# A hybrid decoder trunk: pools re-laid so that matmul blocks begin on 2 KB boundaries in SBUF

## The chip, the cores and the metric

The kernel runs on one core of a Trainium2 chip. The metric is the device time of one execution in microseconds; the median of three runs stands for the kernel. One further execution was recorded by the hardware profiler, and its rows are the ones quoted here. The engines are PE (matrix products), DVE (vector), ACT (scalar), POOL (GpSimd) and SP, which here issues the DMAs.

## The reference

Two layers of a decoder trunk on x of 512 tokens by 1024 features, float32. Each layer normalises x, projects it once into everything that three token mixers need, runs the mixers, merges them through gates, projects the merged rows and adds them to x.

```python
h = rms_norm(x, pre_norm)
z_a, xbc, dt, u, z_b, q_lat, kv_lat, k_rope, z_c, gates = split_columns(h @ w_in)
a = ssd_branch(z_a, xbc, dt, ...) @ w_a        # causal conv, chunked state space scan, gate, norm
b = s5_branch(u, z_b, ...) @ w_b               # complex diagonal scan, gelu, GLU, gate
c = mla_branch(q_lat, kv_lat, k_rope, z_c) @ w_c   # causal attention, 16 heads
merged = sum(sigmoid(gate_i) * branch_i)
x = x + rms_norm(merged @ w_o, post_norm)
```

The SSD branch also uses the small tables `conv_w`, `conv_b`, `d_ssd` and `ssd_norm`, the GLU uses `b_glu`, the latents use `q_norm` and `kv_norm`.

## The kernel before

**Tiling.** Tokens lie along the free axis (512 of them, one PSUM bank), features on the 128 partitions. A float32 product is made of three: each operand is split into a high part `h` (rounded by ACT) and a low part `l` (the rest, by DVE or POOL), and PE forms high x high, high x low and low x high. `dense` does that for a bank: over the 128-row blocks of its input it issues L109 (`wh`, high part) and L110 (`wh`, low part) in turn, then L112 (`wl`, high part). With eight blocks a bank is 24 matmuls of 512 columns. The moving operand is the input block, 512 columns of 4 bytes, so 2 KB per partition: `hh`/`hl` for the normalised x, `ah`/`al` for the activations that the branches leave, `cqh`/`cql` for the MLA latents. The stationary operand is a block of 128 columns of `wh` or `wl`, 512 bytes. `mm3` (L54 to L56) issues the three products for one block; in the output projection it is the weights `woh`/`wol` that move and `ah`/`al` that are stationary. `weight` streams one 128 x 1024 block of weights into `wf`, ACT makes `wh` from it (L59) and DVE (L71) or POOL (L74) makes `wl`; each has two buffers.

**Stages.** In each layer: the norm, the first two tiles of the projection and the MLA branch with the preparation of the S5 matrices as filler work (to about 390 us in layer 0, 1390 in layer 1); the merges of `w_c` beside the S5 scan on DVE (to about 500); the SSD branch (to about 697); eight S5 blocks, each with a tile of the `w_a` merge, and the GLU (to about 885); the `w_b` merges with the loads of the output weights (to about 960); the output projection (to about 1010, and the end).

**What sets the order.** A scheduler orders the instructions of each engine by a simulation of its own, and waits are added to that order; each engine then runs its row in order. SP's DMA queue is such a row as well: a load that waits holds those behind it. Tiles come from pools, and a pool's place in SBUF follows from the pools opened before it. The pools of a stage (`mla`, `act`, `mg`, `dt`, `ssd`, `s5`, `wo`, `scan`) open and close and take over each other's space; a tile waits for the instructions that use the tiles whose addresses it takes over. A tile with a tag in a pool that stays open waits for the readers of the buffer's last holder alone.

**The names that the change touches.** `sm` is the pool of small tiles and stays open for both layers. `qn` and `kvn` are the norms' gains of the latents, `mx` and `nm` the row maxima of the attention; they are in the stage pool `mla`. `cw`, `cb`, `dsk`, `sn` (SSD) are in `mg`, loaded at L703 to L710, and `cw` and `cb` are halved by DVE. `bglu` (L940 to L942) is in `s5` and halved as well. `s5_block.load` (L892) brings a block's inputs `u` and its states `sdr` into a staging tile `uf` or `sf` of the pool `s5`, one buffer each. `tmp` is a pool tag with seven buffers of 128 x 512, used by all stages.

**Where blocks begin.** The addresses of the program before, in bytes past a 2 KB boundary, are: `wf`, `wh`, `wl`, `hh`, `hl` and the tiles of `kp`, `tp` 768; `act` (`ah`, `al`), `mg` and `mla` 640, with the latents' `cqh` and `cql` at 704; `dt` and `s5` 1024; `ssd` 384; `wo` 2016.

Of the kernel before, what the change touches and what calls it, by code (L numbers as in the profile page):

```python
# [9 lines left out]
F32 = mybir.dt.float32  # L10
# [7 lines left out]
L = 2  # L18
# [5 lines left out]
# first tile of each part of the input projection, in the host's order  # L24
ZA, XBC, UB, ZB, CQ, CKV, ZC, GT = 0, 8, 24, 32, 40, 44, 46, 54
SCALE = 96.0 ** -0.5
MAGIC = 12582912.0
SWAP16 = [(i + 16) % 32 for i in range(32)]
# [6 lines left out]
class Trunk:  # L35
    def __init__(self, ctx, tc, a, out, tap=None):
# [3 lines left out]
        self.const = pool("const")  # L40
        self.wp = pool("wp", 2)
# [3 lines left out]
        self.sm = pool("sm")  # L45
# [39 lines left out]
    def weight(self, src, n, pool=None):  # L85
        """hi and lo parts of a block of n columns per partition, streamed from DRAM"""
# [14 lines left out]
    def dense(self, src, rhs, m=P, n=None, main=True):  # L101
        """[m, T] bank of src^T rhs; rhs: (hi, lo) per 128 rows"""
# [12 lines left out]
    def proj2(self, l, tiles):  # L115
        """two tiles of the projection, first for the first half of the tokens"""
# [57 lines left out]
    def sincos_small(self, ang, n):  # L174
# [21 lines left out]
        # sin = 2 s c, cos = 1 - 2 s^2  # L196
# [8 lines left out]
    def rsqrt_mean(self, ss, n, scale, eps=EPS):  # L205
        """(scale * ss + eps) ** -0.5 on n columns"""
        v = self.sm.tile([P, n], F32, name="rs_v", tag=f"rsv{n}")
        r = self.sm.tile([P, n], F32, name="rs_r", tag=f"rsr{n}")
        self.ts(v, ss, scale, eps, ALU.mult, ALU.add)
        self.gt(r, v, self.mhalf[:, :n], ALU.pow)  # L210
        return r

    def rsqrt_rows(self, sq, scale):
        """sq [128, T]: sums over partitions -> (scale * sum + eps) ** -0.5 along T, on every partition"""
# [13 lines left out]
    def s5_prep(self, l, pp):  # L228
# [27 lines left out]
        # f = (abar - 1) / lambda  # L256
# [18 lines left out]
        # coefficients of the scan over blocks: groups 0..31 on the lower half, 32..63 on the upper  # L275
# [25 lines left out]
        def block(b):  # L301
            """inputs in blocks of 8 steps: (step, channel of the group) on partitions; what depends on B and C alone"""
# [49 lines left out]
        def back(b, s, uf, bb, v1, w1):  # L352
# [19 lines left out]
            if s % 2:  # L372
# [3 lines left out]
                # kernel of the steps within a block  # L376
# [32 lines left out]
    def norm_in(self, tt, xt, G):  # L409
        """RMS norm of a tile of tokens (two halves of its features), transposed and split into self.hh, self.hl"""  # L410
# [15 lines left out]
    def silu2(self, l, tile_, keep=True):  # L426
        """2 silu of a tile of the projection"""
# [24 lines left out]
    def merge(self, l, i, w, acts, m, rrow=None):  # L452
        """merged += 2 sigmoid(gate_i) * (w^T acts) (* rrow along T), a tile of it; its gates run ahead"""
# [15 lines left out]
    def mla(self, l, fill):  # L469
        nc, tc, a = self.nc, self.tc, self.a  # L470
        with tc.tile_pool(name=f"mla{l}", bufs=1, reuse_waits="tile") as mp:
            qn, kvn = mp.tile([P, 4], F32, name="qn"), mp.tile([P, 2], F32, name="kvn")
# [118 lines left out]
    def attend_qk(self, mp, q, k, h):  # L591
        """rows of exp(q k^T * SCALE - max), causal; their sums in self.rs"""
        nc = self.nc
        mx, nm = (mp.tile([P, 4], F32, name=x, tag=x, bufs=2) for x in ("mx", "nm"))
# [17 lines left out]
    def attend_v(self, mp, scs, v):  # L612
        """probabilities times v, transposed, as the sum of two parts of [64, T]"""
        nc = self.nc
        # key block kb holds queries kb * 128 ...
# [25 lines left out]
    def ssd_dt(self, l, sp):  # L641
        """dt, its cumulative decays and what depends on tokens and heads alone"""
        nc, a, sm = self.nc, self.a, self.sm
        raw = sp.tile([P, 512], F32, name="dtraw")
        self.act_(raw[32:48], self.krdt[32:48])
# [35 lines left out]
        cs2 = sp.tile([64, 512], F32R, name="cs2")  # L681
# [16 lines left out]
    def ssd(self, l):  # L698
        nc, tc, a = self.nc, self.tc, self.a
        with tc.tile_pool(name=f"ssd{l}", bufs=1, reuse_waits="tile") as sp:  # L700
            dt, cs, cs2, dte, dec = self.dts
            cw, cb = self.mgp.tile([P, 16, 4], F32, name="cw"), self.mgp.tile([P, 16], F32, name="cb")
# [4 lines left out]
            dsk, sn = self.mgp.tile([P, 8], F32, name="dsk"), self.mgp.tile([P, 8], F32, name="sn")  # L707
# [5 lines left out]
            def conv(t):  # L713
                """silu of the causal convolution of a tile of channels"""
# [499 lines left out]
```

## Time and profile before

| | us |
|---|---|
| runs | 2005.52, 2007.95, 2009.80 |
| median | 2007.95 |
| span of the profiled execution | 2005.7 |
| PE busy in it | 1890.3 |
| DVE busy in it | 1451.9 |
| ACT busy in it | 942.0 |
| POOL busy in it | 649.9 |

The span is the time from the first to the last instruction of the one profiled execution; the times of the runs also hold what lies around it. Matmuls are pipelined, so a matmul's duration in the timeline (0.39 us for 512 columns) is longer than the distance to the next one's start; what a stream of matmuls costs is read from the distance of the starts.

### The profile page before, as it was taken

What the parts mean: (1) busy time and instruction counts of PE and PEld (TensorE: products, weight loads), DVE (VectorE), ACT (ScalarE), POOL (GpSimd) and SP (SyncE); (2) the same over time, 40 slices, a digit from 0 to 9 for tenths busy, and PEclk for the clock granted to TensorE, in tenths of its full rate; (3) what the DMA queues carried; (4) which work ended last, traced back from release to release, by engine and by line L of the source; (5) the groups of instructions that cost most, each with busy time, mean ns of one, the idle gap of its engine ahead of it and who ended that gap; (6) DMA issues with size and microseconds to landing.
All of it is one profiled execution on the core that took longest, in us unless ns stands there. A gap on an engine that the chain in (4) does not pass through costs nothing.

```text
span 2005.7 us, 27806 instructions
## 1 busy us (share of the span) xinstructions
PE 1890.3 (94%) x9688; PEld 1524.2 (76%) x9688; DVE 1451.9 (72%) x2845; ACT 942.0 (47%) x1743; POOL 649.9 (32%) x743
## 2 busy tenths in 40 slices
PE   7897999899999989999997999998999999999998
PEld 6685777687877868887875777776878887788786
DVE  7866667699999857744478666677999996776433
ACT  4364566522555445533333655564235563554331
POOL 1855466301333201201118556662013331012010
PEclk9898999899999999999998999998999999999999
DMA  5232234232321266344232333342332224662531
GB/s 166 88 115 83 91 118 128 83 108 74 127 74 64 75 184 181 93 152 157 88 91 83 108 104 111 91 139 82 96 123 77 74 74 111 181 171 84 168 126 42
DMA packets 132605, 219.96 MB, mean 110 GB/s; under 512 B 36208, under 2 KB 75760, under 8 KB 131952
## 3 DMA queue, kind: packets, MB, share of 16 engines
q1 hardware_dynamic: 132464, 218.19, 35.4%
q8 instruction: 76, 1.25, 0.3%
q14 instruction: 65, 0.53, 0.1%
HBM read 182.08 MB, written 31.33 MB: 106 GB/s over the span
## 4 chain that ended last, share of the span: by engine, by line
PE 59%; DVE 25%; DMA 7%; POOL 3%; ACT 3%; issue 2%; SPq 1%; DVEq 0%; POOLq 0%; ACTq 0%
PE mm L109 14%; PE mm L110 13%; PE mm L112 13%; DVE wl L71 4%; DVE keep L62 3%; PE mm L54 2%; PE mm L55 2%; PE mm L56 2%; DMA wf<-in_w_in 2%; DVE ms L882 2%; DVE sc_t L879 2%; PE pk L378 2%; DVE ms L881 1%; PE aux L55 1%; PE aux L54 1%
## 5 line engine op out<-in xcount | busy, mean ns | idle before, releaser
L109 PE MATMUL mm<-hh,wh 128*128 128x512 f32 (+1 forms) x1232 | 501.2, 407 | 16.4 <-DVE ql L71 8.8
L110 PE MATMUL mm<-hl,wh 128*128 128x512 f32 (+1 forms) x1232 | 493.6, 401 | 0.0
L59 ACT ACTIVATE wh<-wf 128x1024 fp32r<-128x1024 f32 (+1 forms) x294 | 291.2, 994 | 423.7 <-PE mm L110 240.8
L71 DVE TENSOR_TENSOR wl<-wf,wh 128x1024 fp32r<-128x1024 f32 (+1 forms) x243 | 297.5, 1229 | 183.8 <-ACT wh L59 149.6
L112 PE MATMUL mm<-hh,wl 128*128 128x512 f32 (+1 forms) x1232 | 315.1, 393 | 2.4 <-DVE wl L71 2.4
L109 PEld LDWEIGHTS mm<-hh,wh 128*128 128x128 f32 (+1 forms) x1232 | 237.2, 193 | 78.6 <-ACT wh L59 10.0
L110 PEld LDWEIGHTS mm<-hl,wh 128*128 128x128 f32 (+1 forms) x1232 | 236.8, 192 | 50.2 <-issue 1.9
L112 PEld LDWEIGHTS mm<-hh,wl 128*128 128x128 f32 (+1 forms) x1232 | 227.5, 187 | 52.0 <-DVE wl L71 3.2
L74 POOL TENSOR_TENSOR mg<-mg,tmp 128x512 f32<-128x512 f32 x32 | 77.7, 2429 | 464.4 <-DVE tmp L71 242.7
L74 POOL TENSOR_TENSOR wl<-wf,wh 128x1024 fp32r<-128x1024 f32 (+1 forms) x51 | 109.5, 2147 | 292.2 <-PE mm L112 186.7
L109 PE MATMUL mm<-ah,wh 128*128 128x512 f32 x512 | 204.1, 401 | 0.1
L110 PE MATMUL mm<-al,wh 128*128 128x512 f32 x512 | 201.2, 394 | 0.0
L112 PE MATMUL mm<-ah,wl 128*128 128x512 f32 x512 | 130.8, 396 | 0.0
L109 PEld LDWEIGHTS mm<-ah,wh 128*128 128x128 f32 x512 | 96.2, 188 | 25.5 <-issue 1.8
L110 PEld LDWEIGHTS mm<-al,wh 128*128 128x128 f32 x512 | 96.2, 188 | 22.1 <-issue 0.5
L112 PEld LDWEIGHTS mm<-ah,wl 128*128 128x128 f32 x512 | 95.7, 188 | 22.6
L602 DVE CUSTOM_DVE_ANT_0 sc<-aux,cmask 128x128 f32<-128x128 f32 (+3 forms) x128 | 60.3, 486 | 50.8 <-PE aux L56 49.1
L59 ACT ACTIVATE sc<-sc,nm 128x128 f32<-128x128 f32 (+3 forms) x128 | 70.3, 553 | 30.3 <-DVE nm L66 30.2
L74 POOL TENSOR_TENSOR pv<-pq,ar 128x288 f32<-128x288 f32 x64 | 56.4, 903 | 85.3 <-PE pk L378 68.3
L71 DVE TENSOR_TENSOR pl<-aux,ph 128x512 fp32r<-128x512 f32 (+1 forms) x96 | 54.8, 594 | 26.2 <-ACT ph L59 25.7
L59 ACT ACTIVATE tmp<-mm 128x512 f32<-128x512 f32 x76 | 44.9, 594 | 60.6 <-PE mm L56 34.1
L62 DVE SCALAR_TENSOR_TENSOR keep<-mm,cw,keep 128x511 f32<-128x511 f32 (+2 forms) x96 | 71.1, 741 | 2.1 <-ACT keep L59 1.5
(344 smaller groups left out, 4079.9 us busy)
## 6 DMA issues: line engine op xcount, KB each, us to landing
wf<-in_w_in SPq DMA_DIRECT2D x156, 512.0 KB
odr<-pv SPq DMA_DIRECT2D x64, 128.0 KB
wf<-in_w_c SPq DMA_DIRECT2D x16, 512.0 KB
wf<-in_w_a SPq DMA_DIRECT2D x16, 512.0 KB
wf<-kpad SPq DMA_DIRECT2D x128, 64.0 KB
wf<-odr SPq DMA_DIRECT2D x16, 512.0 KB
wf<-in_w_glu SPq DMA_DIRECT2D x16, 512.0 KB
wf<-in_w_b SPq DMA_DIRECT2D x16, 512.0 KB
```

Source lines behind the costliest of these rows:

```text
L54: mm(out, ah, bh, start=start, stop=False)
L55: mm(out, ah, bl, start=False, stop=False)
L56: mm(out, al, bh, start=False, stop=stop)
L59: self.nc.scalar.activation(out, in_, func, **kw)
L62: self.nc.vector.scalar_tensor_tensor(out, in0, s, in1, op0, op1)
L71: self.nc.vector.tensor_tensor(out, a, b, op)
L74: self.nc.gpsimd.tensor_tensor(out, a, b, op)
L109: mm(ps[:m], wh[:, o(i)], bh, start=i == 0, stop=False)
L110: mm(ps[:m], wh[:, o(i)], bl, start=False, stop=False)
L112: mm(ps[:m], wl[:, o(i)], bh, start=False, stop=i == k - 1)
L378: nc.tensor.matmul(pk.rearrange("p g k -> p (g k)"), bbp[b % 2][:, q:q + 4].rearrange("p g h -> p (g h)"), v1[:, :, 0:8].rearrange("p g k ...
L602: nc.vector.tensor_tensor_reduce(out=sc, in0=ps[:, :n], in1=self.cmask[:, 512 - n:512], op0=ALU.add, op1=ALU.max, scale=1.0, scalar=-3.0e3 ...
```

## The change

The pool `sm` opens ahead of the large pools. A helper `align` takes a pad tile of a given number of float32 columns from a pool and clears one column of it; it is called in `sm` (200 columns), in the pool `dt` (160) and in `wo` (504). The small tiles `qn`, `kvn`, `mx`, `nm`, `cw`, `cb`, `dsk`, `sn` and `bglu` move from their stage pools into `sm`, each with a tag of its own, so layer 1 uses the same buffer as layer 0. The staging tile of `s5_block.load` becomes a `tmp`. `cs2` is taken from its pool earlier. Comments are dropped, which moves the line numbers.

```diff
         self.const = pool("const")
+        self.sm = pool("sm")
+        self.align(self.sm, PAD_LOW)
         self.wp = pool("wp", 2)
         self.hp = pool("hp")
         self.kp = pool("kp", 8)
         self.tp = pool("tp", 7)
-        self.sm = pool("sm")
...
+    def align(self, pool, n):
+        t = pool.tile([P, n], F32, name="pad", tag="pad")
+        self.nc.vector.memset(t[:, 0:1], 0.0)
...
-            qn, kvn = mp.tile([P, 4], F32, name="qn"), mp.tile([P, 2], F32, name="kvn")
+            qn, kvn = self.sm.tile([P, 4], F32, name="qn", tag="qn"), self.sm.tile([P, 2], F32, name="kvn", tag="kvn")
...
-        mx, nm = (mp.tile([P, 4], F32, name=x, tag=x, bufs=2) for x in ("mx", "nm"))
+        mx, nm = (self.sm.tile([P, 4], F32, name=x, tag=x, bufs=2) for x in ("mx", "nm"))
...
         raw = sp.tile([P, 512], F32, name="dtraw")
+        cs2 = sp.tile([64, 512], F32R, name="cs2")
+        self.align(sp, PAD_DT)
...
-            cw, cb = self.mgp.tile([P, 16, 4], F32, name="cw"), self.mgp.tile([P, 16], F32, name="cb")
+            cw, cb = self.sm.tile([P, 16, 4], F32, name="cw", tag="cw"), self.sm.tile([P, 16], F32, name="cb", tag="cb")
...
-            dsk, sn = self.mgp.tile([P, 8], F32, name="dsk"), self.mgp.tile([P, 8], F32, name="sn")
+            dsk, sn = self.sm.tile([P, 8], F32, name="dsk", tag="dsk"), self.sm.tile([P, 8], F32, name="sn", tag="sn")
...
-            f = sp.tile([P, 8, 64], F32, name=nm + "f", tag=nm + "f")
+            f = self.tmp().rearrange("p (g c) -> p g c", g=8)
...
-        bg = sp.tile([P, 8], F32, name="bglu")
+        bg = self.sm.tile([P, 8], F32, name="bglu", tag="bglu")
...
                 if m < 6:
                     w_out(wp, m)
+            self.align(wp, PAD_TOP)
```

By the addresses of the changed program, `wp`, `hp`, `kp`, `tp`, `act`, `mla`, `mg`, `dt`, `ssd`, `s5` and `wo` all begin at 0 past a 2 KB boundary, and so do their blocks of 2 KB. The pools of the S5 preparation and the scan stay where they were.

The scheduler makes new rows of this. At the start of the program DVE's row was, from the product `pq` of the first S5 tables on (`e_...` is an exponential on small tiles, `hl` the low part of the normalised x):

```order
L66 TENSOR_SCALAR pq_810<-bc_803,sgn 128x128
L66 TENSOR_SCALAR e_nf<-e_t 128x64
L62 SCALAR_TENSOR_TENSOR e_r<-e_nf,e_zc 128x64
L66 TENSOR_SCALAR e_t<-e_nf 128x64
L62 SCALAR_TENSOR_TENSOR e_r<-e_nf,e_r 128x64
L66 TENSOR_SCALAR e_t<-e_t 128x64
L66 TENSOR_SCALAR e_p<-e_r 128x64
L62 SCALAR_TENSOR_TENSOR e_p<-e_p,e_r 128x64 x5
L71 TENSOR_TENSOR hl<-aux,hh 128x4x128
```

and what stands behind `pq` is now:

```order
L75 TENSOR_SCALAR cw<-cw 128x64
L75 TENSOR_SCALAR cb<-cb 128x16
L75 TENSOR_SCALAR e_nf<-e_t 128x64
L71 SCALAR_TENSOR_TENSOR e_r<-e_nf,e_zc 128x64
L75 TENSOR_SCALAR e_t<-e_nf 128x64
L71 SCALAR_TENSOR_TENSOR e_r<-e_nf,e_r 128x64
L75 TENSOR_SCALAR e_t<-e_t 128x64
L75 TENSOR_SCALAR e_p<-e_r 128x64
L71 SCALAR_TENSOR_TENSOR e_p<-e_p,e_r 128x64 x3
L75 TENSOR_SCALAR bglu<-bglu 128x8
L71 SCALAR_TENSOR_TENSOR e_p<-e_p,e_r 128x64
L80 TENSOR_TENSOR hl<-aux,hh 128x4x128
```

The halvings of `cw`, `cb` and `bglu` now stand in it. In SP's row at the same place the loads of layer 0 followed the S5 tables `bc` like this:

```order
L316 DMA bc_803<-in_s_bc 128x256
L317 DMA bc_804<-in_s_bc 64x256
L318 DMA bc_804<-in_s_bc 64x256
L95 DMA wf<-in_w_tail 128x384
L95 DMA wf<-in_w_in 128x1024 x6
```

and now they do like this:

```order
L325 DMA bc_805<-in_s_bc 128x256
L326 DMA bc_806<-in_s_bc 64x256
L327 DMA bc_806<-in_s_bc 64x256
L713 DMA cw<-in_conv_w 128x64
L714 DMA cb<-in_conv_b 128x16
L104 DMA wf<-in_w_tail 128x384
L719 DMA dsk<-in_d_ssd 64x8 x2
L720 DMA sn<-in_ssd_norm 128x8
L104 DMA wf<-in_w_in 128x1024
L951 DMA bglu<-in_b_glu 128x8
```

The loads of `cw`, `cb`, `dsk`, `sn` and `bglu` for layer 0 have moved up among the first weights. At the entry of the first S5 block of layer 0 SP's row was (`kpad` and `odr` are the block's matrices):

```order
L95 DMA wf<-in_w_in 128x1024 x2
L95 DMA wf<-in_w_a 128x1024
L894 DMA uf<-u_570 128x512
L894 DMA sf<-sdr_4583 128x1x512
L93 DMA wf<-kpad_567 16x8x128 x8
L95 DMA wf<-odr_568 128x1024
L894 DMA uf<-u_570 128x512
L894 DMA sf<-sdr_4583 128x1x512
L95 DMA wf<-in_w_in 128x1024 x2
```

and is now:

```order
L104 DMA wf<-in_w_in 128x1024 x2
L719 DMA dsk<-in_d_ssd 64x8 x2
L104 DMA wf<-in_w_a 128x1024
L720 DMA sn<-in_ssd_norm 128x8
L102 DMA wf<-kpad_569 16x8x128 x5
L904 DMA tmp<-u_572 128x512
L904 DMA tmp<-sdr_4585 128x1x512
L102 DMA wf<-kpad_569 16x8x128 x3
L104 DMA wf<-odr_570 128x1024
L904 DMA tmp<-u_572 128x512
L904 DMA tmp<-sdr_4585 128x1x512
L104 DMA wf<-in_w_in 128x1024 x2
```

The loads of `u` and `sdr` have moved behind five of the `kpad` loads, and those of `dsk` and `sn` for layer 1 stand in front of them.

## Rows read from the trace of the kernel before

**Rows 1.** The page: busy time and share of the span; the chain that ended last by engine
```profile
PE 1890.3 (94%) x9688; PEld 1524.2 (76%) x9688; DVE 1451.9 (72%) x2845; ACT 942.0 (47%) x1743; POOL 649.9 (32%) x743
...
PE 59%; DVE 25%; DMA 7%; POOL 3%; ACT 3%; issue 2%; SPq 1%; DVEq 0%; POOLq 0%; ACTq 0%
```

**Rows 2.** Table of stretches: busy us and instructions by engine, clock, DMA share, GB/s
```profile
400.00:500.00 100.00, 98.25 (x430) 78.40 (x430) 95.85 (x326) 26.31 (x33) 7.28 (x3) 1.00 0.27 96
760.00:1010.00 250.00, 249.91 (x1251) 203.25 (x1250) 139.52 (x165) 107.15 (x153) 36.69 (x19) 1.00 0.42 134
```

**Rows 3.** Timeline of PE, 825 to 885 us: start, duration, line, operation, tiles, count
```profile
837.29 1.98 PE L112 MATMUL mm<-hh,wl 128*128 128x512 f32 x8
...
842.73 1.98 PE L112 MATMUL mm<-hh,wl 128*128 128x512 f32 x8
...
859.46 2.03 PE L112 MATMUL mm<-ah,wl 128*128 128x512 f32 x8
...
865.06 2.03 PE L112 MATMUL mm<-ah,wl 128*128 128x512 f32 x8
```

**Rows 4.** Timeline of PE in w_out, 960 to 985 us
```profile
968.17 0.40 PE L54 MATMUL mm<-woh,ah 128*128 128x512 f32 x1
...
970.97 0.40 PE L54 MATMUL mm<-woh,ah 128*128 128x512 f32 x1
```

**Rows 5.** Timeline of PE in layer 0's MLA stage, 243 to 250 us
```profile
247.19 0.39 PE L109 MATMUL mm<-cqh,wh 128*128 128x512 f32 x1
...
248.59 0.39 PE L109 MATMUL mm<-cqh,wh 128*128 128x512 f32 x1
```

**Rows 6.** PE's groups by line and shape: count, busy us, mean ns, idle before
```profile
L109 PE MATMUL mm<-ah,wh 128*128 128x512 f32 x512 | 204.1, 401 | 0.1
...
L54 PE MATMUL mm<-woh,ah 128*128 128x512 f32 x128 | 49.9, 395 | 0.0
...
L109 PE MATMUL mm<-cqh,wh 128*128 128x512 f32 x96 | 42.8, 450 | 1.1 <-ACT cqh L59 1.0
```

**Rows 7.** Timeline of DVE at the start, 20 to 60 us
```profile
26.27 0.29 DVE L66 TENSOR_SCALAR pq<-bc,sgn 128x128 f32<-128x128 f32 x1 [2.84 <-DMA bc<-in_s_bc]
...
28.63 0.68 DVE L71 TENSOR_TENSOR hl<-aux,hh 128x512 fp32r<-128x512 f32 x1
```

**Rows 8.** Timeline of SP's DMA queue at the S5 entry, 684 to 722 us
```profile
697.69 0.56 SPq L894 DMA_DIRECT2D sf<-sdr  x1
698.31 7.36 SPq L93 DMA_DIRECT2D wf<-kpad  x8
...
707.33 1.49 SPq L95 DMA_DIRECT2D wf<-in_w_in  x2
```

**Rows 9.** Waits of SP's queue, 680 to 760 us: total, times, longest
```profile
SPq L894 <- PE aux L218: 6.7, 1, 6.7
```

**Rows 10.** Timeline of PE at the S5 entry, 712 to 722 us
```profile
718.38 0.50 PE L109 MATMUL mm<-hh,wh 128*128 128x512 f32 x1 [3.06 <-ACT wh L59]
...
719.89 0.63 PE L110 MATMUL mm<-hl,wh 128*128 128x512 f32 x1
720.32 0.63 PE L109 MATMUL mm<-hh,wh 128*128 128x512 f32 x1
```

**Rows 11.** Timeline of PE at the S5 entry of layer 1, 1700 to 1740 us
```profile
1705.45 0.51 PE L109 MATMUL mm<-hh,wh 128*128 128x512 f32 x1 [3.56 <-ACT wh L59]
```

**Rows 12.** Timeline of SP's DMA queue at the start, 0 to 60 us
```profile
19.12 0.65 SPq L316 DMA_DIRECT2D bc<-in_s_bc  x1
...
24.86 0.53 SPq L95 DMA_DIRECT2D wf<-in_w_tail  x1
```

**Rows 13.** Timeline of SP's DMA queue before the SSD stage, 376 to 402 us
```profile
381.45 0.42 SPq L703 DMA_DIRECT2D cw<-in_conv_w  x1
...
382.39 1.13 SPq L709 DMA_DIRECT2D dsk<-in_d_ssd  x2
```

**Rows 14.** Timeline of DVE before the SSD stage, 376 to 402 us
```profile
385.28 0.18 DVE L66 TENSOR_SCALAR cw<-cw 128x64 f32<-128x64 f32 x1
```

More of the change, by code (lines that the diff above doesn't have):

```diff
@@ L27 @@
 MAGIC = 12582912.0
+PAD_LOW = 200
+PAD_DT = 160
+PAD_TOP = 504
 SWAP16 = [(i + 16) % 32 for i in range(32)]
@@ L680, in ssd_dt @@
         self.act_(cst[0:16], ps[:16])
-        cs2 = sp.tile([64, 512], F32R, name="cs2")
         self.split(cst[0:32], cs2[0:32], cs2[32:64])
```

## The prediction, made before the result was known

> **What bounds the kernel now.** I read the page first, then a table of busy time by stage, then the starts of single matmuls in PE's timeline. The page says that PE is the engine to look at: it is busy for 1890.3 us of the span and makes 59% of the chain that ended last, with DVE at 25% [rows 1]. The stage table says where that holds: from 760 to 1010 us PE is busy for 249.91 of 250 us; in the merges of 400 to 500 us it still shows 98.25, but DVE, which runs the S5 scan there, has 95.85 [rows 2]. So a cheaper matmul shortens the tails of both layers one for one, and the merges of 400 to 500 us hardly.
>
> The change is about addresses, so the next question is whether a matmul's period depends on its address today. By the address table of the program before, the moving blocks hh and hl begin 768 bytes past a 2 KB boundary, the activations ah and al at 640, the MLA latents cqh and cql at 704, the output weights at 2016. Every one of these 512-column blocks is 2 KB long and so crosses a boundary; the stationary weights wh and wl begin at 768, and one block of four crosses.
>
> The timeline has the periods. A bank is 24 matmuls of 512 columns. Two banks of hh start their last eight matmuls 842.73 - 837.29 = 5.44 us apart, 226.7 ns each. Two banks of ah: 865.06 - 859.46 = 5.60 us, 233.3 ns each [rows 3]. In w_out twelve matmuls take 970.97 - 968.17 = 2.80 us, 233.3 ns [rows 4]; with cqh six take 248.59 - 247.19 = 1.40 us, 233.3 ns [rows 5]. So there are two levels, 6.7 ns apart, though all four kinds cross a boundary alike. What the faster kind has for itself is that its moving and stationary blocks share one offset (768 and 768); ah differs from its weights by 128 bytes, cqh by 64. After the change all of these begin at 0: they share an offset, and none crosses.
>
> **The change, term by term.**
>
> *Tail matmuls.* There are 512 matmuls with ah or al on each of three lines, and 128 with the output weights on each of three [rows 6]. A quarter of the former belongs to the merges of 400 to 500 us and their twin in layer 1, where DVE ends last; that leaves 3 x 384 + 3 x 128 = 1,536, or 64 banks, where PE ends last. At 5.60 - 5.44 = 0.16 us a bank [rows 3] this is 10.2 us if each falls to the level of hh. The other end is 0: the level may depend on something that the change leaves alone. I take 7, since the S5 blocks cut banks up with 64- and 128-column matmuls, and a stream that is cut need not settle at once.
>
> *MLA.* The latents' 96 matmuls on each of three lines [rows 6] save 288 x 6.7 ns = 1.9 us; PE ends last for about half of these stages, so 1. For hh and hl I take nothing: they have the lower level already.
>
> *S5 entry.* Today the staging tile of the first S5 block lies on the SSD stage's last tile: SP waits 6.7 us for a matmul of that stage [rows 9] before it issues the load at 697.69, then 7.36 us of eight kpad loads, then w_in at 707.33 [rows 8]. PE pays with 3.06 us of idle time until wh is ready [rows 10], and 3.56 us at the same place in layer 1 [rows 11]. After the pause matmuls of 512 columns start 0.43 us apart (719.89, 720.32) instead of 0.23 [rows 10], the lower clock level; eight of them at 0.2 us more are 1.6 us. After the change the load goes to the shared temporaries, which have long been free, and that wait leaves the head of the queue. In layer 0, however, the reloads of dsk and sn for layer 1 now stand in front of it and wait for the last readers of layer 0's copies; in layer 1 nothing does. The bounds: 0 if sn holds the queue as long as the old wait did; 3.06 + 3.56 + 2 x 1.6 = 9.8 us if all goes. I take 4: little in layer 0, most of it in layer 1. What is late next there is w_in's own load, the last thing before wh.
>
> *Start.* The small tables now have one buffer for both layers, and layer 0's loads have nothing to wait for, so they rise to the start of the program: on SP cw and cb stand ahead of w_tail, which issues at 24.86 today [rows 12]; on DVE their halving stands right behind pq, and that of bglu inside the exponential's chain. DVE runs in order, so that chain and the last hl split queue behind these loads, PE's second half of the first projection waits for hl, and POOL's S5 preparation for the chain. Today pq ends at 26.56 and hl starts at 28.63 [rows 7]. A cw load was issued at 381.45 [rows 13] and its halving ran at 385.28 [rows 14], 3.8 us later. Issued at 24.86, cw is there at about 28.7, 2.1 us after pq. Behind it SP issues cb, w_tail, two dsk, sn and one w_in, about 0.55 us each [rows 12, 13]; so bglu goes out at about 28.6 and is there at 32.4, while a DVE that is 2.1 us late reaches its halving at about 30.3: another 2.1. I take 4 for both, as PE has little else to do when that chain is late. The other ends: 0, if the loads land sooner than the one at 381 did; 6, if PE's pause also costs it a piece at the lower clock.
>
> *What costs nothing.* The reloads of qn, kvn, cw, cb and bglu for layer 1 stand on SP's queue behind loads that issue later than their readers end, and ahead of nothing that is due at once. The five pads are five DVE memsets of one column; at cw's 0.18 us [rows 14] each, under 1 us in all, beside DVE work that waits for PE. The cs2 tile moves in its pool without an instruction.
>
> *Order.* The scheduler has put layer 1's MLA stage in another order. I know of no side that this favours and take 0, within 4 either way.
>
> *Sum.* -7 - 1 - 4 + 4 = -8. The profiled execution's span was 2005.7 us, so 1997.7; the median of the runs, 2007.95, is 2.25 above that span, so the time is **2000.0 us**, 0.40% less. What a measurement of this kernel can tell from no change is about 0.2%, 4 us.
>
> **The rivals.**
>
> *Nothing from alignment.* The two levels may come from something else that differs between these streams, not from offsets. For it: hh crosses a 2 KB boundary in every block and has the lowest period, so crossing as such cannot be the cost. Against it: ah, cqh and the output weights sit in three pools, are written by different stages, and show the one slower level. Then -4 + 4 stays, with the order's 4 either way: about 2008. By the Trainium skill's "SBUF — State Buffer", section "Who interferes with whom", PE never waits on anyone for its reads of SBUF, and its section "Operand start alignment" makes a start address a matter of legality and not of speed; by that page this rival is right, but it has no reason for the two levels in [rows 3].
>
> *A lower level.* 226.7 and 233.3 are 6.7 ns apart; if blocks that begin on a boundary take away one more such step, all of the hh and hl matmuls gain too. The program has 3,696 of 512 columns; with two thirds of them on PE-bound time they give 3,696 x 6.7 ns x 2/3 = 16.5 us, and the tail's 1,536 fall by two steps, 20.6 instead of the 7 taken: 2000 - 16.5 - 13.6 = 1970. Nothing in the trace shows a 512-column stream that settles below 226.7, and that speaks against it. [...]
>
> *The start costs more than alignment gives.* One mechanism: DVE stands still behind cw and bglu at 26 to 36 us, the S5 preparation behind it slips, PE runs dry and takes the next piece at the lower clock. If these loads take the 7.1 us of bc there (it went out at 19.12 [rows 12] and its reader began at 26.27 [rows 7]) instead of 3.8, DVE waits 5.4 us for cw and 2.0 for bglu, 7.4 in all, and with 1.6 for the clock the start costs 9. With 3 from the tail and nothing from the S5 entry the time is 2007.95 - 3 + 9 = 2014. It decides from the point where a cw load needs some 6 us.
>
> **How the numbers follow.** Forecast 0.50, its own range 1994 to 2006 from the bounds of its terms; 0.38 of it is below 2003.9 and 0.12 within 0.2%. Nothing from alignment 0.20: 0.03, 0.12 and 0.05 for faster, same and slower. A lower level 0.13, all of it faster; 0.05 of that goes to the lowest time named there. The start 0.17: 0.05 same, 0.12 slower. Together faster 0.54, same 0.29, slower 0.17. The range goes from 1985, which leaves out most of the lower level (about 0.1), to 2012, which leaves out the upper part of the slow case (about 0.1).
>
> **What would show it.** Right: two ah banks in the tail 5.44 us apart, and w_out's twelve matmuls in 2.72; SP's first S5 load without a wait for a matmul; DVE idle for some 2 us near 27 us. Wrong: ah banks still at 5.60 (first rival); hh banks below 5.44 (second); PE idle for more than 8 us longer in the first 100 us than before (third); or layer 1's MLA stage longer or shorter by over 5 us from its order alone, which I could not size.

## The result: 2040.65 us, 1.6% slower

The changed kernel takes 2040.65 us (median of 4 runs, 2038.01 to 2042.21), the kernel before 2007.51 beside it; the ratio is 1.0163, 95% interval 1.0148 to 1.0177. The forecast was 2000.0 in a range of 1985 to 2012. The profiled execution's span is 2038.8 us, 33.1 above the one of before.

The page of the changed kernel (busy time and share of the span; then the chain that ended last by engine and by line):

```profile
PE 1897.2 (93%) x9688; PEld 1544.4 (76%) x9688; DVE 1445.1 (71%) x2850; ACT 939.9 (46%) x1743; POOL 648.3 (32%) x743
...
PE 54%; DVE 24%; DMA 10%; POOL 3%; issue 3%; SPq 3%; ACT 2%; DVEq 0%; POOLq 0%; ACTq 0%
PE mm L118 13%; PE mm L119 12%; PE mm L121 12%; DMA tmp<-sdr 4%; DVE wl L80 4%; DVE keep L71 3%; PE mm L64 2%; PE mm L63 2%; PE mm L65 2%; SPq L102 2%; POOL pv L83 1%; DVE tmp L71 1%; DVE tmp L80 1%; PE pk L387 1%; DVE sc_t L889 1%
```

PE was 59% of the chain [rows 1] and is 54%; DMA has gone from 7% to 10%, and a transfer that was not among the lines before, the S5 states' load into a temporary (`tmp<-sdr`), alone makes 4%, some 80 us. PE is busy about as long as before, and it waits more. Two things of opposite sign stand in that sum: the periods below are shorter, and the mean granted clock is 0.958 where it was 0.970. By its two levels, 1.2 and 2.4 GHz, that is, as an estimate, 171 us at the lower level (8.4% of 2038.8) instead of 120 (6.0% of 2005.7), and matmuls start 0.43 us apart there instead of 0.23 [rows 10]. So some of the 33 us may lie in PE's own work; how much was not separated.

**The matmuls did what was forecast.** PE's timeline in the GLU of layer 0 (start, duration):

```profile
863.57 1.98 PE L121 MATMUL mm<-hh,wl 128*128 128x512 f32 x8
869.00 1.98 PE L121 MATMUL mm<-hh,wl 128*128 128x512 f32 x8
...
885.33 1.98 PE L121 MATMUL mm<-ah,wl 128*128 128x512 f32 x8
890.76 1.98 PE L121 MATMUL mm<-ah,wl 128*128 128x512 f32 x8
```

Two banks of ah are now 5.43 us apart and two of hh 5.43; they were 5.60 and 5.44 [rows 3]. The lower level is reached, and hh has not gone below it.

**Where the time went.** The starts of the same matmuls in both traces give the places: layer 0 is 6.3 us late at the first matmul of the latents (`cqh`) and 8.9 us late at the first matmul of the S5 blocks (718.6 against 709.7); the eight blocks add 17.4 us more, and 4.3 come back from the GLU to the end of w_out. Layer 1 loses 4.2 us up to its S5 blocks and 10.6 in them, and 3.9 come back. The table of stretches says the same of PE:

```profile
760.00:860.00 100.00, 88.55 (x570) 73.69 (x569) 58.77 (x64) 43.53 (x62) 10.99 (x5) 0.95 0.42 127
860.00:1035.00 175.00, 174.94 (x779) 144.65 (x779) 92.31 (x115) 70.04 (x103) 30.08 (x17) 1.00 0.37 125
```

From the GLU on PE is full again, as in [rows 2]; in the S5 blocks before it PE is busy for 88.55 of 100 us, where it was full from 760 us on.

**The S5 blocks.** SP's queue in the changed kernel has a row of this kind for the fifth, sixth and seventh block of each layer; `kpad` are a block's padded kernel tables, which become its weights, `u` its inputs, `sdr` its states. Here the loads of block 7's kpad with block 6's u and sdr behind them, then block 8's kpad (start, duration of the issue):

```profile
796.71 4.08 SPq L102 DMA_DIRECT2D wf<-kpad  x7
800.84 0.43 SPq L904 DMA_DIRECT2D tmp<-u  x1
801.37 0.50 SPq L904 DMA_DIRECT2D tmp<-sdr  x1
...
820.46 4.25 SPq L102 DMA_DIRECT2D wf<-kpad  x7
```

And the kernel before in the same place:

```profile
783.12 0.80 SPq L93 DMA_DIRECT2D wf<-kpad  x2
783.97 0.51 SPq L894 DMA_DIRECT2D sf<-sdr  x1
...
800.43 0.80 SPq L93 DMA_DIRECT2D wf<-kpad  x2
```

A block took 17.3 us (783.12 to 800.43) and takes 23.8 (796.71 to 820.46). In the kernel before, from the third block on, a block's states go out after two of its own kpad loads, and its inputs ahead of those; each waits only for the split of the block before to leave the one staging buffer. Now both stand behind seven kpad loads of the *next* block. The chain of the changed kernel shows that this closes a loop:

```profile
796.71 0.33 SPq L102
...
801.37 8.27 DMA tmp<-sdr
809.66 0.64 ACT sh L68
810.32 0.69 DVE sl L80
...
819.30 1.14 DVE wl L80
820.46 0.33 SPq L102
...
825.28 8.24 DMA tmp<-sdr
```

The first kpad load of block 8 waits for the buffer that the split of block 7's kpad weights releases, with their low part `wl` (819.30 + 1.14 = 820.44; it issues at 820.46). The states of block 7 go out only behind all seven, as those of block 6 did one turn earlier, 801.37 - 796.71 = 4.7 us after the first. They land 8.3 us later and are split (`sh`, `sl`); and since DVE runs in order, the next kpad weights' `wl` comes after that split, and releases the next kpad load. So a block's states wait for the weights of the block they belong to, and the weights of the block after it wait for these states. No matmul stands in this piece of the chain.

**The start.** DVE's timeline of the changed kernel:

```profile
27.76 0.29 DVE L75 TENSOR_SCALAR pq<-bc,sgn 128x128 f32<-128x128 f32 x1 [3.59 <-DMA bc<-in_s_bc]
28.38 0.20 DVE L75 TENSOR_SCALAR cw<-cw 128x64 f32<-128x64 f32 x1 [0.34 <-DMA cw<-in_conv_w]
...
33.98 0.17 DVE L75 TENSOR_SCALAR bglu<-bglu 128x8 f32<-128x8 f32 x1 [3.54 <-DMA bglu<-in_b_glu]
...
34.19 0.68 DVE L80 TENSOR_TENSOR hl<-aux,hh 128x512 fp32r<-128x512 f32 x1
```

DVE stands for 0.34 us on cw and for 3.54 on bglu, 3.9 in all, and hl, which started at 28.63 [rows 7], starts at 34.19; PE waits for it:

```profile
34.93 0.39 PE L64 MATMUL mm<-hl,wh 128*128 128x256 f32 x1 [3.80 <-DVE hl L80]
```

### The profile page after: what moved, and what is told of

It is laid out like the page before. It is cut to its first block, busy times and chain, and to the rows that moved or that the text cites. A ratio compares the mean times of both kernels' runs of the same rounds, so it can differ in the third digit from the quotient of the medians.

```text
span 2038.8 us, 27765 instructions
## 1 busy us (share of the span) xinstructions
PE 1897.2 (93%) x9688; PEld 1544.4 (76%) x9688; DVE 1445.1 (71%) x2850; ACT 939.9 (46%) x1743; POOL 648.3 (32%) x743
## 4 chain that ended last, share of the span: by engine, by line
PE 54%; DVE 24%; DMA 10%; POOL 3%; issue 3%; SPq 3%; ACT 2%; DVEq 0%; POOLq 0%; ACTq 0%
PE mm L118 13%; PE mm L119 12%; PE mm L121 12%; DMA tmp<-sdr 4%; DVE wl L80 4%; DVE keep L71 3%; PE mm L64 2%; PE mm L63 2%; PE mm L65 2%; SPq L102 2%; POOL pv L83 1%; DVE tmp L71 1%; DVE tmp L80 1%; PE pk L387 1%; DVE sc_t L889 1%
## 5 line engine op out<-in xcount | busy, mean ns | idle before, releaser
L118 PE MATMUL mm<-ah,wh 128*128 128x512 f32 x512 | 199.8, 393 | 0.0
```

Source lines behind the costliest of these rows:

```text
L118: mm(ps[:m], wh[:, o(i)], bh, start=i == 0, stop=False)
```

## The experiments

Times stand beside runs of the kernel before on the same chip; the ratio is to those.

**First: which of the three losses is which.** Three edits of the change could each slow it: the staging tile, the tables, the new addresses. k1 puts back the first (it needs 32 bytes, so the low pad shrinks), k2 the second, k3 both; k4 makes the first edit alone on the kernel before.

```diff
# k1: on the changed kernel
-PAD_LOW = 200
+PAD_LOW = 192
-            f = self.tmp().rearrange("p (g c) -> p g c", g=8)
+            f = sp.tile([P, 8, 64], F32, name=nm + "f", tag=nm + "f")
-            self.align(wp, PAD_TOP)
# k2: on the changed kernel, with PAD_LOW = 304
-            cw, cb = self.sm.tile(...)          dsk, sn = self.sm.tile(...)
+            cw, cb = self.mgp.tile(...)         dsk, sn = self.mgp.tile(...)
-        bg = self.sm.tile([P, 8], F32, name="bglu", tag="bglu")
+        bg = sp.tile([P, 8], F32, name="bglu")
# k3: staging and tables back, PAD_LOW = 192, and the pad in wo stays, PAD_TOP = 104
# k4: on the kernel before
-            f = sp.tile([P, 8, 64], F32, name=nm + "f", tag=nm + "f")
+            f = self.tmp().rearrange("p (g c) -> p g c", g=8)
```

> The changed kernel with the S5 staging tiles uf and sf back in the stage's pool, one buffer each; to find the 32 bytes that this needs, the low pad is 192 columns, so that all large pools begin at 2016 past a 2 KB boundary, moving and stationary blocks still at one common offset, but every 2 KB block crosses a boundary. Theory 'staging' (seven kpad loads now stand ahead of a block's states on SP's queue in S5 blocks 5 to 7): the S5 blocks go back to their length of before and the time falls by 26 to 30 us from 2040.7, to 2011 to 2015; what is left above before is the start. Rival 'addresses' (the new places of the tiles slow the S5 blocks): no change, 2035 to 2043. On the period of matmuls: if the common offset is what counts, banks with ah stay at 5.44 us; if the 2 KB boundary is what counts, they are back at 5.60.

> The changed kernel with cw, cb, dsk and sn back in the merges' pool and bglu back in the S5 pool (their loads can't be issued at the program's start), the pads set so that wp, hp, act, mla, mg and wo still begin on 2 KB boundaries; the staging tiles stay the shared temporaries. Theory 'staging plus tables': the first 100 us are back at the length of before, so the time falls by 5 to 9 us from 2040.7, to 2032 to 2036, and the S5 blocks stay slow. Rival 'tables do it all' (the reloads of dsk, sn and bglu hold SP's queue and so slow the S5 stage): 2005 to 2015. Rival 'order of the start is chance': no change, 2038 to 2043.

> Both put back: tables in the merges' and the S5 pool, staging tiles in the S5 pool; what is left of the change is that qn, kvn, mx and nm lie in sm, and that moving and stationary blocks of the large matmuls share one offset (1600 past a 2 KB boundary, not on it). Theory 'common offset': both losses go and the shorter matmul period stays: 1998 to 2003, faster than before. Theory 'boundary': without the boundary the period is as before: 2005 to 2010. If the S5 stage or the start is slow here too: above 2010, and neither the staging nor the tables are the cause.

> The kernel before with one edit: the S5 staging tile is a shared temporary. No address and no table moves. Theory 'staging': the S5 blocks 5 to 7 lengthen by 16 to 18 us in layer 0 and 10 to 13 in layer 1: 2030 to 2038. Rival 'addresses': as before, 2005 to 2010.

| | us | ratio to before, 95% interval |
|---|---|---|
| k1, staging back | 2019.97 | 1.0051 (1.0031 to 1.0070) |
| k2, tables back | 2034.18 | 1.0127 (1.0103 to 1.0152) |
| k3, both back | 2016.02 | 1.0042 (1.0029 to 1.0055) |
| k4, before with the staging in temporaries | 2029.53 | 1.0104 (1.0081 to 1.0127) |

k4 settles the staging: the edit alone, with no pad and no table, costs 1.04%, 21 us, and k1 gives the same 21 back (2040.65 - 2019.97 = 20.7). k4's queue has the loop of the changed kernel too: seven kpad loads ahead of u and sdr, at 781.77 and again at 805.61, 23.8 us a block. Both effects are smaller than I expected (k1 2011 to 2015, k4 2030 to 2038): some of what I had put down to the staging is what k1 still has above before. k2 gives 6.5, or 0.36% by the ratios, as theory had it for the tables. k3 speaks against both theories that stood behind it: 2016 is neither 1998 to 2003 nor 2005 to 2010. Something else in the change costs time. Its banks of ah had the lower level, though its pools begin at 1600 past a boundary; so had k1's, at 2016. The 2 KB boundary is not what the matmuls want.

**What a matmul's period depends on.** A kernel of matmuls alone measures pairs of start addresses.

```python
for m, s in [(0, 0)] + PAIRS:   # bytes past a 2 KB boundary: moving, stationary; N is 96
    ...
    for i in range(N):
        k = i % 8
        a, b = m // 4 + k * 512, s // 4 + k * P
        nc.tensor.matmul(ps, st[:, b:b + P], mv[:, a:a + 512], ...)
```

> Matmuls alone, none of the trunk's computation: for each of 51 pairs of start addresses (moving block and stationary block, bytes past a 2 KB boundary) a run of 96 matmuls of 512 moving and 128 stationary float32r columns that walk over eight blocks each; a row's length over 96 is the period. Theory 'common offset': the period depends on the difference of the two offsets alone: low at (0, 0), (640, 640) and (768, 768), higher at a difference of 64, 128, 640 or 96. Theory 'boundary': low at a moving offset of 0 whatever the stationary offset, higher for every other moving offset, (768, 768) and (640, 640) included. Theory 'nothing from addresses': one period for all pairs. If the lowest period is 226.7 ns here as in the kernels, nothing else in the kernels slows their best matmuls; if it is near 216, the kernels' other traffic costs the rest.

PE's timeline of it (the name holds the two offsets; a period is the distance to the next row's start over 96):

```profile
77.89 22.48 PE L43 MATMUL m0x_s128x<-mv,st 128*128 128x512 f32 x96
100.20 21.93 PE L43 MATMUL m0x_s256x<-mv,st 128*128 128x512 f32 x96
121.97 22.56 PE L43 MATMUL m0x_s320x<-mv,st 128*128 128x512 f32 x96
...
320.57 21.94 PE L43 MATMUL m640x_s128x<-mv,st 128*128 128x512 f32 x96
342.35 22.48 PE L43 MATMUL m640x_s256x<-mv,st 128*128 128x512 f32 x96
364.66 22.56 PE L43 MATMUL m640x_s320x<-mv,st 128*128 128x512 f32 x96
387.06 22.55 PE L43 MATMUL m640x_s512x<-mv,st 128*128 128x512 f32 x96
409.44 21.95 PE L43 MATMUL m640x_s640x<-mv,st 128*128 128x512 f32 x96
431.23 22.47 PE L43 MATMUL m640x_s768x<-mv,st 128*128 128x512 f32 x96
453.54 22.47 PE L43 MATMUL m640x_s1024x<-mv,st 128*128 128x512 f32 x96
...
807.78 22.14 PE L43 MATMUL m64x_s0x<-mv,st 128*128 128x512 f32 x96
829.76 22.57 PE L43 MATMUL m96x_s0x<-mv,st 128*128 128x512 f32 x96
```

(0, 256) takes 121.97 - 100.20 = 21.77 us, 226.8 ns a matmul; (640, 640) and (640, 128) take 227.0 and 226.9. (640, 768), the offsets of ah and its weights before, takes 453.54 - 431.23 = 22.31 us, 232.4 ns; (0, 128) the same. In all 51 pairs the lower level, 226.7 to 227.2 ns, stands where the two offsets differ by a multiple of 256 bytes, whatever they are themselves, and the others have 229 to 234 ns. The theory of the common offset comes nearest of the three on record: what it says of its own pairs came out, but the offsets need only agree modulo 256. And 226.7 is the lowest with nothing else running, as in the kernel [rows 3], so no sign is left that the other engines and the DMAs take anything from the kernels' best matmuls.

**Offsets alone, in the kernel.** x1 is the kernel before with three pads that bring each large pair of blocks level modulo 256, with PE, ACT, POOL and SP in the order of before (DVE has the pads' memsets more, and one instruction two places later); x2 does the opposite to hh.

```diff
# x1: on the kernel before
+        self.align(self.sm, 32)        # act and all above it by 128 bytes
+            self.align(mp, 48)         # the latents
+            self.align(wp, 56)         # the output weights
# x2: on the kernel before, a pool of one pad between the weights and hh
+        self.wpp = pool("wpp")
         self.hp = pool("hp")
+        self.align(self.wpp, 32)
```

> The kernel before with three pads and no other edit (32 columns at the end of sm, 48 behind kvn, 56 in the pool of the output weights): hh, hl, wh, wl, ah, al stay or come to 768 past a 2 KB boundary, the latents to 1024, the output weights to 1792, so moving and stationary blocks differ by a multiple of 256 bytes in every large matmul, and nearly all blocks still cross 2 KB boundaries. The order of instructions is that of the kernel before on PE, ACT, POOL and SP; DVE has five one-column memsets more. Theory 'difference modulo 256': banks with ah fall to 5.44 us, w_out to 226.7 ns a matmul; each layer's tail loses 3 us and the MLA stages about 1: 2000 to 2003, ratio 0.996 to 0.998. Rival 'the 2 KB boundary': no change, 2006 to 2010.

> The kernel before with a pad of 32 columns behind the weights: hh and hl go to 896, 128 bytes off their weights, and ah and al to 768, level with them. Order of instructions as before. Theory 'difference modulo 256': banks with hh rise to 5.60 us and banks with ah fall to 5.44; of 3,696 matmuls some two thirds are on PE-bound time, 3,696 x 5 ns x 2/3 = +12, less 5 from ah: 2013 to 2018. Rival 'the 2 KB boundary': no change, since no block begins on one before or after: 2006 to 2010.

x1: 2003.53 us, ratio 0.9972 (0.9961 to 0.9983). x2: 2012.12, ratio 1.0022 (1.0009 to 1.0034). PE's timeline of x1, and then of x2, in the GLU:

```profile
840.94 1.98 PE L117 MATMUL mm<-hh,wl 128*128 128x512 f32 x8
846.38 1.98 PE L117 MATMUL mm<-hh,wl 128*128 128x512 f32 x8
...
862.70 1.98 PE L117 MATMUL mm<-ah,wl 128*128 128x512 f32 x8
868.14 1.98 PE L117 MATMUL mm<-ah,wl 128*128 128x512 f32 x8
```

```profile
839.67 2.03 PE L118 MATMUL mm<-hh,wl 128*128 128x512 f32 x8
845.27 2.03 PE L118 MATMUL mm<-hh,wl 128*128 128x512 f32 x8
...
856.22 1.98 PE L118 MATMUL mm<-ah,wl 128*128 128x512 f32 x8
861.66 1.98 PE L118 MATMUL mm<-ah,wl 128*128 128x512 f32 x8
```

In x1 both are 5.44 us apart; in x2 they have changed places, hh at 5.60 and ah at 5.44. So 128 bytes move the period either way. x1's 5.6 us (0.28% of 2008) are what the offsets alone are worth in this kernel. x2 came out 1 us below its expected stretch; that more of the hh matmuls than I took have other work ending last would explain it, and was not shown.

**What else the change costs.** k3 was 0.42% above before although its losses were put back. PE runs its matmuls in another order than before in several hundred places of the trace; without the pad in the pool dt (x4) it has the order of before.

```diff
# x3: on the kernel before
         raw = sp.tile([P, 512], F32, name="dtraw")
+        self.align(sp, 160)
# x4: on k3
-        self.align(sp, PAD_DT)
# x7: on the kernel before
         raw = sp.tile([P, 512], F32, name="dtraw")
+        sp.tile([P, 160], F32, name="pad", tag="pad")
```

> The kernel before with one pad of 160 columns in the pool dt, its one-column memset among the first instructions of the SSD stage. No offset between a moving and a stationary block of the large matmuls changes, but the scheduler lays out 435 rows of PE and 270 of DVE in another order (end of layer 0's MLA, its SSD stage, layer 1's MLA). Theory 'what is left above before in the version with both put back is this pad's order': +7 to +11, 2015 to 2019, with +3 to +5 in layer 0's SSD entry. Rival 'the rest comes from where the small tables and the low pools lie': no change, 2006 to 2010.

> The version with tables and staging put back, without the pad in dt; its order of instructions is the one of the kernel before but for a few rows of SP and the memsets. Theory of the pad's order: the common offset's gain is left alone, 2000 to 2003. Rival: 2011 to 2017 as with the pad.

> The kernel before with the 160-column pad in the pool dt as in the last version with that pad, but without the one-column memset that goes with it: the addresses of the SSD stage are the same as there, the order of instructions is the one of the kernel before on all engines. Theory 'the memset makes the scheduler lay out another order, and the order costs the time': 2006 to 2010, no change. Rival 'the SSD tiles' new addresses cost it': 2015 to 2020 as with the memset.

| | us | ratio to before, 95% interval |
|---|---|---|
| x3, the dt pad with its memset | 2018.50 | 1.0049 (1.0033 to 1.0064) |
| x4, k3 without the dt pad | 2007.58 | 0.9995 (0.9981 to 1.0010) |
| x7, the dt pad without its memset | 2006.83 | 0.9996 (0.9982 to 1.0009) |

By the addresses of the two programs, which the traces do not show, x3 and x7 lay out the SSD stage alike. They differ by one DVE memset of one column in each layer, which stands here in x3's row, at the end of the MLA stage:

```text
TENSOR_TENSOR pl<-aux,ph 128x256
MEMSET pad 128x1
MEMSET dtraw 32x512
TENSOR_TENSOR pml<-pm,pmh 128x256
```

With it, the scheduler lays out the rest of the stage otherwise: from there on x3's trace has instructions in another order on all five engines (435 rows of PE by the count on record), where x7's has the order of before on every one. The first S5 matmul starts at 714.3 instead of 709.7 us, with the last one of layer 1 at 1823.8 instead of 1813.5. These are the extremes of one group in the view of a tile (min, median and max ns of one, then first and last start), before and then x3:

```profile
L54 PE MATMUL pM<-wh,uh x128: 220/223/274, 709.7 to 1813.5; 128*64 128x128 f32 x128
```

```profile
L58 PE MATMUL pM<-wh,uh x128: 220/223/308, 714.3 to 1823.8; 128*64 128x128 f32 x128
```

So the memset costs some 10 us through the order that it brings about, and the new addresses nothing. Which wait of the new order costs it was not followed. x4 is below its rival, but also 4 to 5 us above the 2000 to 2003 of its theory: it has x1's periods and not x1's gain. Its ten runs have a mean of 2007.3 us and x1's twelve, on the same chip, 2002.9; with a spread of 2 to 3 us in each that is no accident. What takes the gain there, with qn, kvn, mx and nm still in sm, other pool offsets and a few of SP's rows moved, stays open.

**Why staging in the temporaries costs 21 us.** In the changed kernel the states go out last, behind the kpad loads and the inputs; x5 puts back their tile alone, and x8 does that with the tables back and no memset in dt, so all three losses would be mended if that were enough.

```diff
# x5: on the changed kernel; x8: the same on k2, with the dt pad's memset left out
-            f = self.tmp().rearrange("p (g c) -> p g c", g=8)
+            f = sp.tile([P, 8, 64], F32, name=nm + "f", tag=nm + "f") if nm == "s" else self.tmp().rearrange(...)
```

> The changed kernel with the staging tile of the states alone (sf) back in the S5 pool; that of the inputs stays a shared temporary, all pools stay on 2 KB boundaries. SP's row again has two kpad loads ahead of the states from the third block on, not seven. Theory 'states behind the kpad loads': the S5 blocks get back 16 to 18 us in layer 0 and about 10 in layer 1 less what the inputs cost, so 2012 to 2020. Rival 'any use of the shared temporaries': 2030 or more.

> The changed kernel with all three losses mended: the states' staging tile in the S5 pool, cw, cb, dsk, sn and bglu in their stages' pools, the pad in dt without its memset; wp, hp, act, mla, mg and wo on 2 KB boundaries, dt, ssd and s5 384 bytes past one. Theory 'three orders cost what the addresses gain': 2000 to 2006, as with the three pads alone (ratio 0.996 to 0.999). If something else of the change costs time: above 2008. If the 2 KB boundary gives something beyond the common offset: below 1999.

x5: 2036.16, ratio 1.0140 (1.0113 to 1.0167). x8: 2025.54, ratio 1.0087 (1.0060 to 1.0114). Both miss their theory: x5 gives back only 4 us of the 21 and lies in the stretch of its rival, "any use of the shared temporaries". So "the states behind seven kpad loads" is not the reason, or not the whole of it. The chain of x5 shows what took their part:

```profile
802.73 7.21 DMA tmp<-u
...
820.77 0.33 SPq L102
...
823.85 7.00 DMA tmp<-u
```

The states are back behind two of their own block's kpad loads. Now the inputs' load, still in a temporary, stands behind five kpad loads and the states of the next block, and closes the same loop at 823.85 - 802.73 = 21.1 us a block. Either the place in SP's row costs the time, whichever load has it, or a temporary as such. x9 keeps the temporaries and only asks for both loads one block ahead; x10 also has the tables back and no memset in dt.

```diff
# x9: on the changed kernel (x10: on k2 without the dt pad's memset)
+    def s5_fetch(self, l, b):          # u and sdr of block b into two temporaries
+        ...
+            f = self.tmp().rearrange("p (g c) -> p g c", g=8)
+            self.nc.sync.dma_start(f, src)
...      (in s5_block; load now only splits)
-        uh, ul = load(u2[b]..., "u")
-        sh, sl = load(self.sdr[...], "s")
+        uf, sf = self.s5_ahead.pop(b)
+        uh, ul = load(uf, "u")
+        sh, sl = load(sf, "s")
+        if b < 7:
+            self.s5_fetch(l, b + 1)
```

> The changed kernel with one edit: the loads of a block's inputs and states into the shared temporaries are asked for one block ahead, so that on SP's row they stand before or among the kpad loads of the block before their own. Staging in the temporaries, tables and pads stay. Theory 'a late place in SP's row' (a load that stands behind the kpad loads can't be issued before the last weights of the block before are split, and its own landing then comes on top): the S5 blocks go back to about their length of before, 2015 to 2023. Rival 'the shared temporaries as such' (their buffers come free late, whatever the place): the blocks stay long, 2032 or more.

> As the last, with cw, cb, dsk, sn and bglu also back in their stages' pools and the dt pad without its memset: staging in the temporaries, but one block ahead, and wp, hp, act, mla, mg and wo on 2 KB boundaries. Theory 'a late place': the common offset's gain is left, 2000 to 2006. Rival 'the shared temporaries as such': 2022 or more, as the version with the states alone put back.

x9: 2014.84, ratio 1.0037 (1.0024 to 1.0050). x10: 1999.50, ratio 0.9956 (0.9943 to 0.9969). x9 gives back 26 us with the temporaries in place, so their buffers are not the cause: the place in the row is. (The edit also puts other rows in another order, so the step from the place to the time rests on the chains above as well. And the 26 us are against the changed kernel; against k1, with the staging tile put back, the intervals overlap.) SP's queue of x9:

```profile
792.91 2.69 SPq L102 DMA_DIRECT2D wf<-kpad  x6
795.65 0.43 SPq L901 DMA_DIRECT2D tmp<-u  x1
796.13 0.51 SPq L901 DMA_DIRECT2D tmp<-sdr  x1
...
813.12 2.69 SPq L102 DMA_DIRECT2D wf<-kpad  x6
```

The loads still stand behind six kpad loads. But in these last blocks they are kpad loads of the same block, where the changed kernel has those of the next one, so the loads go out a whole block earlier; in blocks 2 to 5 they stand with the block before, ahead of all kpad loads of their own. My expectation had them there throughout. A block now takes 813.12 - 792.91 = 20.2 us at this place. x10 has the lowest time of all versions, 0.44% below before and 2.0% below the changed kernel. Its interval overlaps x1's; if it is better than x1, it may be by its S5 blocks, which are 2.1 and 2.3 us shorter than before in the two layers of its profiled execution, where x1's are 1.9 longer and 0.4 shorter. That was not taken apart further.

## Why the prediction was wrong, step by step

**What was right.** *Tail matmuls*: forecast from the distance of ah banks, 5.60 to 5.44 us; measured 5.43. The rivals "nothing from alignment" and "a lower level" are both ruled out by that row and by m1: hh stays at 5.43, and 226.7 ns is the lowest in any of the 51 pairs. *Tail and MLA, -8*: x1 gives -5.6 us for both (0.28%, interval 0.17 to 0.39%, 3.4 to 7.8 us), so the term was sized too high; the GLU to the end of w_out gives back 3 to 4 us in each layer, and the MLA stages little. One thing that the term left out is on record: x1's runs have a mean granted clock of 0.965 and those of before beside them 0.969, by the two levels some 15 us more at the lower one, as an estimate. How much of the gain that takes back was not separated. *Start, +4*: right in place and near in size, in part by luck. The two waits came to 0.34 and 3.54 us, where 2.1 and 2.1 were forecast (the cw load needed 2.1 us from its issue, bglu 3.4), so the sum fits and its halves do not. At the first matmul of the latents the tables cost 4.8 us (6.3 late in the changed kernel, 1.5 in k2); over the whole program 0.36%, 7 us, by k2, but only 0.09% by k1 against k3, where the staging is put back.

**The step that failed: the S5 entry's "the load goes to the shared temporaries, which have long been free", -4.** It was worked out from buffers alone and for the first block alone. There SP does not wait for the SSD stage's matmul any more, but dsk and sn hold the queue in its place, as the bounds allowed:

```profile
SPq L719 <- DVE tmp L71: 3.9, 1, 3.9
SPq L720 <- DVE tmp L75: 2.5, 1, 2.5
```

The wait that was removed was 6.7 us [rows 9]; the two that stand there now are 6.4, and PE's idle time is 2.75 and then 3.30 us where it was 3.06 [rows 10]. In layer 1, where most of the 4 was booked, the 3.56 us [rows 11] are gone, but PE waits 4.55 us at 1736.89 for the weights of a kpad block in their place. So the entry gave nothing. The large part lay outside the step: from the fifth block on the loads stand behind seven kpad loads of the next block, in a loop that DVE and SP close without PE, and in place of -4 the edit costs 21 us (k4, k1). The temporaries were free, as I said: from 690 to 870 us no load of u or sdr waits longer than 0.9 us for anything once its turn has come. SP's row is what put the load late. The prediction read that row at the entry and no further: the excerpt ahead of it is the first block's, where the kpad loads in front of u are the block's own.

**The other step: "Order: I know of no side that this favours and take 0, within 4 either way".** It was 10 us (x3 against x7), to the slow side, and the pads that "cost nothing" brought it: a memset of 0.1 us was priced by its duration, and its price was the order that the scheduler makes with it. Of that no bound could be had from the trace of before; an order that differs in hundreds of places should have widened the range on its own.

**The balance.** By ratios, in per cent of the kernel before: offsets -0.28 (x1), tables +0.36 (changed kernel less k2), the dt pad's memset +0.49 (x3), staging +1.04 (k4): +1.61, where +1.63 was measured. That it fits so closely is luck: the four intervals together leave some 0.4 either way, and k3 (+0.42) and x4 (-0.05) lie about 0.2 above what the same terms give for them (+0.21 and -0.28). The slow rival of the prediction named the start as its mechanism; the start paid about what was forecast, and the slowness came from where a gain had been booked and from an order that had been put at nothing.

## What to carry to other kernels

Where a tile moves to another pool under a scheduler, read the queue's row in every repetition of the loop and not at its entry alone, and ask of each load what stands in front of it, when that is released, and whether the load's own landing closes a loop; asking for the loads one block ahead was worth 26 us of the changed kernel's time here. Put padding in without an instruction, or look whether the instruction moves others. Before blocks are re-laid for alignment, measure the period against the offsets in a kernel of matmuls alone: here three small pads (x1) gave the shorter periods that the whole re-layout was for.

## What the runs showed of the hardware

A float32r matmul of 512 columns, each with a stationary block of its own, starts every 226.7 ns at best, even with nothing else running (m1, at a granted clock of 0.998), and every 229 to 234 ns where its moving and stationary blocks' start addresses differ by something that is no multiple of 256 bytes. Which of the two it is does not depend on 2 KB boundaries or on where the blocks lie themselves (m1, x1, x2). The height of the upper one does: (64, 0) takes 829.76 - 807.78 = 21.98 us, 229.0 ns, and (640, 320), which differs by 64 modulo 256 as well, 387.06 - 364.66 = 22.40 us, 233.3 ns, as cqh had before with its stationary block 64 bytes above the moving one [rows 5]. Why the addresses of two operands meet at all was not tried.
